# Rows of the modulation on the vector engine, and a router packed into column groups, in a two-layer diffusion backbone

## The chip, the cores and the metric

The kernel runs on one core of a Trainium2 chip. The metric is the device time of one execution in microseconds (us), from runs of the whole program; 0.2% of it are 5.8 us. TensorE (PE), VectorE (DVE), ScalarE (ACT), GpSimd (POOL) and SyncE (SP, which issues most transfers) each work through a queue of their own in order.

## The reference, cut to what matters

1024 latent tokens and 256 context tokens of 1024 features go through two layers. Each layer has six modulation rows per kind of token, a product of a vector with a 1024 by 6144 matrix (24 MB per layer), and an expert layer with 16 experts that each choose 128 latent tokens.

```
for layer in range(2):
    mod  = silu(c) @ mod_w[layer] + mod_b[layer];  sh1, sc1, g1, sh2, sc2, g2 = split(mod, 6)
    modc = silu(c_ctx) @ mod_w[layer] + mod_b[layer]         # the same for context tokens
    h = rms_norm(x, norm1_g) * (1 + sc1) + sh1               # rows 0 and 1
    y = conv_and_latent_attention(h) if layer == 0 else windowed_attention(h)
    x = x + g1 * (y @ w_out)                                 # row 2
    h2 = rms_norm(x, norm2_g) * (1 + sc2) + sh2              # rows 3 and 4
    aff = softmax(h2 @ router_w[layer])                      # 16 experts
    g, idx = top_k(aff.T, 128)
    x = x + g2 * scatter_add(idx, g * expert(h2[idx]))       # row 5
out = rms_norm(x, final_g)
```

In layer 1 the context tokens end with their keys and values, so their rows 2 to 5 of that layer are not needed.

## The kernel before, in words

The order of the work of every engine is written out by hand: inside `tc.manual_schedule` each queue holds its instructions in program order. float32 operands are split in a high and a low part, and `mm3` (line 162) makes three products of them (lines 163 to 165). Weights arrive in a ring of buffers, are copied to their high part by ScalarE, and the low part is a subtraction on VectorE (or GpSimd).

**Modulation.** A `Part` (class at line 277) makes two rows for both kinds of tokens on TensorE: for each of 8 pieces of 128 features (1 MB) four products into four groups of 32 columns (line 299). A `Row` (class at line 324) makes one row on VectorE: for each of four pieces of 256 features (1 MB) two multiply-adds over [128, 1024] per kind of tokens (line 348; the first is line 350), and at its end `sum` adds over the partitions with one product per half and kind, with a matrix of ones (line 356), an addition on VectorE, and a store by GpSimd. `modulations` merges the pieces of both into one generator: its first call loads two pieces ahead and each later one uses a piece and loads another. Before, `PARTS` are layer 0's rows 2 to 5 and layer 1's rows 0 and 1 for both kinds; `ROWS` are layer 1's rows 2 to 5 for latent tokens. Layer 0's rows 0 and 1 come ahead of the convolution.

**Convolution** (from line 559). Four chunks of 128 features, each with 15 projections of 256 tokens (24 products, lines 163 to 165): five groups of tokens by u, gate c and gate b. `proj` ends with one call of the generator, in all 54 calls for 44 pieces. After the last z (line 613) of a chunk VectorE has the taps (lines 579 to 581), the gates (line 585) as their projections end, and the low parts of the next chunk's weights (line 488), which the next chunk's first product reads.

**Output, router and route** (`mixer_out`, line 1252). Tiles of 128 tokens; a generator `steps(j)` puts pieces of tile j−1's router between tile j's products. `R` (line 1244) multiplies the tokens (128x128 weights) with 16 router columns, 8 products per tile. The softmax over all tiles (`softmax_experts`, line 1442) stands at the head of `route_x`, which finds each expert's 128 tokens with VectorE. `W.convert` (line 1084) splits expert weights ahead, on GpSimd where it is given `pool`.

**Layer 1's projections** (`layer1_mixer`, loop from line 1979). Ten tiles of 128 tokens, in the order of seven latent ones, context, latent, context. For each: the output of layer 0's last expert is added for the tile two on (`P`, `add`), with squares and the norm (lines 1876 to 1888, 172 to 189); the transposes and split of the next tile (`turn`, lines 393 and 1904); products `M` with three thirds of the weights, 24 products each (keys and values first), and the rotation of keys (`kv`) and queries (`q`, lines 1921 to 1925).

```
if j:
    x.M(range(8), 2)
    tiles[j - 1].q(1)
for y in x2:
    y.add(); y.sq(); y.norm()
x.kv()
if not x.s:                       # latent tokens
    if j: x.M(range(8), 0)
    x.q(0)
    if j: x.M(range(8), 1)
```

`early` (line 2233) brings layer 1's rows 0 and 1 onto the partitions inside an expert of layer 0, and the router's weights (`load_routers`, line 1418) with them.

Of the kernel before, what the change touches and what calls it, by code (L numbers as in the profile page):

```python
# [21 lines left out]
D = 1024  # L22
# [17 lines left out]
# one step of the software pipeline of an attention: (operation, how many steps late)  # L40
# [55 lines left out]
def hybrid_block_kernel(ctx, tc, A, out, dbg=None, upto=99):  # L96
# [13 lines left out]
    def psum(name, **tags):  # L110
        """PSUM of a phase: tag -> (buffers, banks each)"""
# [20 lines left out]
    act.copy(identb, ident)  # L132

    warm = const.tile([128, 1], F32, name="warm")

    def table(f, src=ones):
        """has the table of a function loaded ahead of its use"""
# [29 lines left out]
    def rstd_steps(pool_, ss, n, dim, tag, out=None):  # L167
        """1/sqrt(ss/dim + eps) for ss [128, n]: the root of dim times 1/sqrt(ss + dim*eps). A generator"""
# [42 lines left out]
    def scale_rows(pool_, l, s, i, g):  # L211
        """norm_g * (1 + sc) on all partitions"""
# [8 lines left out]
    def columns(c, n, scratch, tag):  # L221
        """n rows of D features with the features on partitions: c [128, row, 8]"""
# [4 lines left out]
    class Ring:  # L227
        """buffers for what is read from DRAM, in turn"""
# [4 lines left out]
        def more(self, raws):  # L233
            """further buffers, next in turn"""
# [11 lines left out]
    class Ahead:  # L246
        """the output projection of the first layer in four parts, the first of them split ahead"""
# [29 lines left out]
    class Part:  # L277
        """two of the rows, for latent and context tokens, 512 features at a time, summed by TensorE"""
# [45 lines left out]
    class Row:  # L324
        """one of the rows, for the kinds of tokens ss, summed by VectorE but over the partitions"""

        def __init__(self, c, l, r, ss, pool_):
            self.c, self.l, self.r, self.ss, self.pool = c, l, r, ss, pool_
            self.w = {}
# [10 lines left out]
        def use(self, k):  # L340
# [3 lines left out]
            for i in range(2):  # L344
                for s, a in zip(self.ss, self.acc):
                    cv = self.c[:, 2 * (k + i) + s:2 * (k + i) + s + 1]
# [5 lines left out]
        def sum(self):  # L352
            n = 64 * len(self.ss)
            pm, mb = bank("C", "pm"), self.mb
# [10 lines left out]

    def modulations(parts, rows, ahead):
        """a generator that stops after every piece of the weights, loaded some pieces ahead"""
# [19 lines left out]
    def transposes8(src, n=8):  # L387
        """eight [128,128] blocks of src (free) into two banks"""
# [8 lines left out]
    # ================= layer 0: projections =================  # L397
    def layer0_conv(hp, wp, cp):
        """first norm, input projection and short convolution"""
        hT = [[hp.tile([128, 8, 256], F32R, name=f"hT{g}_{i}") for i in range(2)] for g in range(5)]  # L400
        csil = hp.tile([128, 16], F32, name="csil")
# [9 lines left out]
        class Group:  # L411
            """256 tokens"""
# [14 lines left out]
            def norm(self):  # L427
                """a generator"""
# [16 lines left out]
            def T(self, b, tag="B"):  # L445
                """two blocks of 128 features of the normalized tokens, features on partitions"""
# [26 lines left out]
        class Chunk:  # L473
            """columns of the input projection, 256 features at a time"""
# [23 lines left out]
        def aside():  # L498
            """the next of the small operations that run between others"""
# [55 lines left out]
        rest = modulations([Part(cs, l, i, cp) for l, i in PARTS], [Row(csil, l, r, ss, cp) for l, r, ss in ROWS], 2)  # L555

        # short conv, 128 features at a time
        for j in range(4):
# [9 lines left out]
            def proj(f, g):  # L568
# [4 lines left out]
                if j or g > 1:  # L573
                    next(rest, None)
# [57 lines left out]
        if "conv" in dbg:  # L632
            for j in range(4):
                pool.dma_start(dbg["conv"][j], yTd[j])
        return hT, chunks[4], rest

    def latents(lp, hT, w, rest, kvT, kT, latT):
        """low-rank queries, keys and values, token-major, and their transposes"""
# [7 lines left out]
        class Latent:  # L646
# [18 lines left out]
            def norm(self):  # L665
                """a generator"""
# [59 lines left out]
    def layer0_mixer():  # L726
# [20 lines left out]
        with sbuf("l0a") as ap_, sbuf("l0t") as tp:  # L747
# [5 lines left out]
            class Head:  # L753
                """k^T and q^T of a head, in pieces of one bank"""
# [120 lines left out]
            with sbuf("l0b") as bp, psum("l0s", S=(2, 2), M=(1, 1), T=(2, 1), O=(1, 1)):  # L875
                class Pair:
                    """attention of 256 latent queries of one head, as the steps of MLA_ORDER"""
# [98 lines left out]
                class Few(Pair):  # L976
                    """attention of the 256 context queries of one head, to context keys only"""
# [72 lines left out]
    class Weights:  # L1050
        """expert weights of a layer in the order of their use: loaded ahead, split in two parts"""
# [43 lines left out]
    # ================= output projection, residual, second norm, router =================  # L1095
    class OutWeights:
        """the output projection in four parts, the first of them loaded ahead"""
# [20 lines left out]
        def first(self, y):  # L1118
            """the first tile of what the weights multiply, in two parts; y to hold it"""
# [1310 lines left out]
```

## Time and profile before

| | |
|---|---|
| median of three runs | 2921.93 us (2921.34 to 2925.74) |
| span of the profiled execution | 2924.6 us, granted TensorE clock 0.966 |
| TensorE busy | 2732.1 us (93%) |
| VectorE busy | 2126.5 us (73%) |
| ScalarE, GpSimd busy | 1609.2 us (55%), 443.8 us (15%) |
| DMA | 613.91 MB, mean 210 GB/s |

The profiled execution's own time is given by its span alone, from its first to its last instruction; it lies 2.7 us above the median of the runs. A line of a timeline gives the start, how long the instruction or group took, engine, line, operation, tiles and, in brackets, the idle time before it and what ended it. Matmuls overlap in their durations, so what one costs is read from the starts of its neighbours. The stages, by the timeline: convolution 40 to 264 us, latents to 310, latent attention to 655, output of layer 0 to 780, route to 845, experts of layer 0 to 1655, projections of layer 1 to 1840, windowed attention to 2142, output to 2257, route to 2305, experts of layer 1 to the end.

### The profile page before, as it was taken

What the parts mean: (1) busy time and instruction counts of PE and PEld (TensorE: products, weight loads), DVE (VectorE), ACT (ScalarE), POOL (GpSimd) and SP (SyncE); (2) the same over time, 40 slices, a digit from 0 to 9 for tenths busy, and PEclk for the clock granted to TensorE, in tenths of its full rate; (3) what the DMA queues carried; (4) which work ended last, traced back from release to release, by engine and by line L of the source; (5) the groups of instructions that cost most, each with busy time, mean ns of one, the idle gap of its engine ahead of it and who ended that gap; (6) DMA issues with size and microseconds to landing.
All of it is one profiled execution on the core that took longest, in us unless ns stands there. A gap on an engine that the chain in (4) does not pass through costs nothing. (4 is left out here: it accounts for less than half of the span.)

```text
span 2924.6 us, 43411 instructions
## 1 busy us (share of the span) xinstructions
PE 2732.1 (93%) x16999; PEld 2160.2 (74%) x16999; DVE 2126.5 (73%) x3298; ACT 1609.2 (55%) x2390; POOL 443.8 (15%) x293
## 2 busy tenths in 40 slices
PE   6999899999959999999999899899998599999996
PEld 5889899988746666666666678688877488877775
DVE  4653799986666666666666554799976688888887
ACT  4201577773225555555555543588943377776664
POOL 2100100000050111010011210232200622221103
PEclk8999999999979999999999999799999799999998
DMA  7782000016438878788888631310056599999994
GB/s 266 286 317 88 5 8 10 9 60 232 159 111 311 290 275 276 273 290 273 276 270 276 227 126 73 128 37 30 25 192 239 197 377 384 383 382 370 367 354 144
DMA packets 274637, 613.91 MB, mean 210 GB/s; under 512 B 25064, under 2 KB 72928, under 8 KB 270336
## 3 DMA queue, kind: packets, MB, share of 16 engines
q1 hardware_dynamic: 259408, 567.38, 54.2%
q0 software_dynamic: 14880, 43.62, 5.8%
q8 instruction: 134, 2.20, 0.3%
q14 instruction: 71, 0.58, 0.1%
q10 hardware_dynamic: 144, 0.13, 0.0%
HBM read 549.41 MB, written 61.67 MB: 209 GB/s over the span
## 5 line engine op out<-in xcount | busy, mean ns | idle before, releaser
L1081 DVE TENSOR_TENSOR wl<-raw,wh 128x2048 fp32r<-128x2048 f32 (+1 forms) x382 | 861.9, 2283 | 247.7 <-ACT wh L1080 247.6
L1080 ACT CAST wh<-raw 128x2048 fp32r<-128x2048 f32 (+1 forms) x392 | 735.5, 1903 | 260.9 <-PE pg L1723 150.2
L1719 PE MATMUL pg<-wl,xh 128*128 128x512 f32 x512 | 210.0, 410 | 3.6 <-ACT xh L159 2.9
L1721 PE MATMUL pu<-wl,xh 128*128 128x512 f32 x512 | 206.1, 402 | 5.3 <-DVE wl L1081 5.3
L1720 PE MATMUL pg<-wh,xh 128*128 128x512 f32 x512 | 203.2, 397 | 0.0
L1724 PE MATMUL pu<-wh,xl 128*128 128x512 f32 x512 | 202.5, 395 | 0.0
L1723 PE MATMUL pg<-wh,xl 128*128 128x512 f32 x512 | 201.8, 394 | 0.0
L1722 PE MATMUL pu<-wh,xh 128*128 128x512 f32 x512 | 201.6, 394 | 0.0
L1775 PE MATMUL pd<-wl,hh 128*128 128x512 f32 x480 | 197.1, 411 | 1.2
L1776 PE MATMUL pd<-wh,hh 128*128 128x512 f32 x480 | 194.0, 404 | 0.0
L1664 POOL DMA_INDIRECT xg<-h2x,gp x32 | 56.5, 1766 | 721.9 <-PE ptr L393 710.1
L1779 PE MATMUL pd<-wh,hl 128*128 128x512 f32 x480 | 151.2, 395 | 0.0
L1739 ACT ACTIVATE sil<-pg 128x512 f32<-128x512 f32 x64 | 38.3, 598 | 204.3 <-PE pg L1723 204.3
L163 PE MATMUL pc<-hT,wh 128*128 128x256 f32 x480 | 139.8, 291 | 5.5 <-ACT wh L487 3.8
L1789 POOL DMA_INDIRECT acc_x<-yo,gp x30 | 92.9, 3096 | 312.4 <-DVE yo L1788 302.2
L164 PE MATMUL pc<-hT,wh 128*128 128x256 f32 x480 | 135.0, 281 | 0.0
L165 PE MATMUL pc<-hT,wl 128*128 128x256 f32 x480 | 134.9, 281 | 0.0
L1719 PEld LDWEIGHTS pg<-wl,xh 128*128 128x128 f32 x512 | 96.5, 188 | 44.9 <-issue 21.6
L1736 PE MATMUL pcg<-raw,cT 128*32 128x256 f32 x2048 | 125.5, 384 | 0.5 <-DMA raw<-in_exp_w_up_dram 0.5
L1775 PEld LDWEIGHTS pd<-wl,hh 128*128 128x128 f32 x480 | 90.1, 188 | 43.6 <-issue 18.9
L1721 PEld LDWEIGHTS pu<-wl,xh 128*128 128x128 f32 x512 | 96.7, 189 | 32.8 <-DVE wl L1081 10.8
L943 ACT CAST pt<-ppt 128x512 fp32r<-128x512 f32 (+1 forms) x192 | 95.1, 516 | 39.0 <-PE ppt L936 36.8
(437 smaller groups left out, 6638.4 us busy)
## 6 DMA issues: line engine op xcount, KB each, us to landing
raw<-in_exp_w_gate_dram SPq DMA_DIRECT2D x128, 1024.0 KB
raw<-in_exp_w_up_dram SPq DMA_DIRECT2D x128, 1024.0 KB
raw<-in_exp_w_down_dram SPq DMA_DIRECT2D x128, 1024.0 KB
raw<-in_mod_w_dram SPq DMA_DIRECT2D x48, 1024.0 KB
yT<-yTd SPq DMA_DIRECT2D x17, 512.0 KB
acc_x<-xn SPq DMA_DIRECT2D x16, 512.0 KB
h2x<-h SPq DMA_DIRECT2D x16, 512.0 KB
raw<-in_w_in_dram SPq DMA_DIRECT2D x8, 768.0 KB
```

The lines of the kernel that those rows point to most:

```text
L163: pe.matmul(o, ah, bl, start=first, stop=False)
L1080: act.copy(wh[:, cs], raw[:, cs])
L1081: (eng or dve).tensor_sub(wl[:, cs], raw[:, cs], wh[:, cs].bitcast(F32))
L1719: pe.matmul(pg, xh[:, k], gl[:, j], start=k == 0, stop=False)
L1720: pe.matmul(pg, xh[:, k], gh[:, j], start=False, stop=False)
L1721: pe.matmul(pu, xh[:, k], ul[:, j], start=k == 0, stop=False)
L1722: pe.matmul(pu, xh[:, k], uh[:, j], start=False, stop=False)
L1723: pe.matmul(pg, xl[:, k], gh[:, j], start=False, stop=k == 7)
L1724: pe.matmul(pu, xl[:, k], uh[:, j], start=False, stop=k == 7)
L1775: pe.matmul(pd[n], hh[k // 4][:, k % 4], w[2][:, k % 2, ns], start=k == 0, stop=False)
L1776: pe.matmul(pd[n], hh[k // 4][:, k % 4], w[1][:, k % 2, ns], start=False, stop=False)
L1779: pe.matmul(pd[n], hl[k // 4][:, k % 4], w[1][:, k % 2, ns], start=False, stop=k == 7)
```

## The change

Layer 0's rows 2 to 5 leave TensorE for VectorE in the convolution, for both kinds of tokens, and pieces come at every second projection (28 pieces in 29 calls). Layer 1's rows 2 to 5 move from the convolution to layer 1's projections, with up to three calls a tile and one load ahead; two tiles of the ring's second pool are lent as accumulators. The router's weights become the stationary operand, padded to 32 columns, in four column groups; a product `F` with `fold` adds the four and transposes. Each tile's softmax follows at once. Two of GpSimd's splits in each route move: in layer 0 one to the route's head and one to VectorE behind it, in layer 1 two of four to VectorE behind it. Layer 1's router weights are loaded and scaled in layer 1's output stage.

```diff
-PARTS = [(0, 1), (0, 2), (1, 0)]
-ROWS = [(1, r, (0,)) for r in (2, 3, 4, 5)]
+PARTS = [(1, 0)]
+ROWS = [(0, r, (0, 1)) for r in (3, 4, 2, 5)]
+ROWS_NEXT = [(1, r, (0,)) for r in (3, 4, 2, 5)]
...
                 if j or g > 1:
-                    next(rest, None)
+                    calls[0] += 1
+                    if calls[0] % 13 % 2 == 0:
+                        next(rest, None)
...
         def R(self):
+
+            p = bank("B", "plT")
+            for k in range(8):
+                q = k % 4 * 32
+                pe.matmul(p[q:q + 32, :128], self.o.router[self.s][:, k], self.xT[:, k], start=k < 4, stop=k >= 4)
+            self.lT = self.wp.tile([128, 128], F32, tag="rb", bufs=2, name="lT")
+            act.copy(self.lT, p[:, :128])
+
+        def F(self):
+
             lg = self.o.lg
             if self.s not in lg:
                 lg[self.s] = bank("C", "lg")
-            c0 = self.i * E
-            for k in range(8):
-                pe.matmul(lg[self.s][:, c0:c0 + E], self.xT[:, k], router[self.o.l, self.s][0][:, k], start=k == 0, stop=k == 7)
+            self.lg = lg[self.s][:, self.i * E:(self.i + 1) * E]
+            pe.matmul(self.lg, self.lT, fold, start=True, stop=True)
+
+        def soft(self):
+
+            a = self.o.aff[self.s][:, self.i, :]
+            m, d = [self.wp.tile([128, 1], F32, tag=t, bufs=2, name=t) for t in ("rm", "rd")]
+            dve.scalar_tensor_tensor(a, self.lg, self.o.rr[self.s][:, self.i:self.i + 1], router[self.o.l, self.s][1],
+                                     op0=ALU.mult, op1=ALU.add)
+            dve.tensor_reduce(m, a, axis=AX.X, op=ALU.max, negate=True)
+            act.activation(a, a, AF.Exp, bias=m, accum_out=d)
+            dve.reciprocal(d, d)
+            dve.tensor_scalar(a, a, d, None, op0=ALU.mult)
...
+                for _ in range(4):
+                    next(m0)
+                    yield
+                y.F()
+                if not y.s:
+                    y.soft()
                 yield from m0
...
-                elif l == 0:
-                    W.convert(1, pool)
...
                 rest = steps(8)
-                take(rest, 15)
+                take(rest, 20)
 
                 def more():
+                    yield
+                    W.convert(1, pool)
                     yield from rest
...
                     yield from rest
-                    for _ in range(4):
-                        for _ in range(12):
-                            yield
+                    for _ in range(2):
+                        yield
                         W.convert(1, pool)
                         W.load(1)
...
             run(fill)
+            if l:
+                W.convert(2)
+                W.load(2)
             if l == 0:
-                W.convert(1, pool)
+                W.convert(1)
...
+                lender = next(p for p, _ in ring.raws if p is not raw0)
+                ring.less(lender)
+                lent = Lent(lender.tile([128, 2, D], F32, tag="raw", bufs=2, name="lent"))
+                rest = modulations([], [Row(l, r, ss, lent, "B") for l, r, ss in ROWS_NEXT], 1)
...
+                    if j:
+                        steps(rest, 1)
                     x.kv()
+                    if j > 1:
+                        steps(rest, 1 if j < TT - 1 else 99)
...
                         x.q(0)
                         if j:
+                            steps(rest, 1)
                             x.M(range(8), 1)
```

## Rows read from the trace of the kernel before

**Rows 1.** Windows: convolution, layer 1's projections; us, busy us per engine, granted clock, DMA share, GB/s.

```profile
40.00:264.00 224.00, 222.24 (x1774) 192.93 (x1775) 126.00 (x247) 44.15 (x84) 20.99 (x31) 0.98 0.65 237
...
1655.00:1840.00 185.00, 171.43 (x762) 136.70 (x760) 95.51 (x231) 80.89 (x150) 16.16 (x12) 0.96 0.33 119
```

**Rows 2.** Windows of 10 us, 1700 to 1830, summed over all thirteen.

```profile
sum 130.00, PE 130.00 PEld 106.22 DVE 66.33 ACT 53.67 POOL 2.71; mean PE 10.00 PEld 8.17 DVE 5.10 ACT 4.13 POOL 0.21
```

**Rows 3.** Timeline of TensorE, convolution, a part's group; start us, us (ends modelled).

```profile
143.75 0.28 PE L165 MATMUL pc<-hT,wl 128*128 128x256 f32 x1
143.96 1.07 PE L299 MATMUL pm<-raw,cs 128*32 128x512 f32 x8
...
145.18 0.28 PE L164 MATMUL pc<-hT,wh 128*128 128x256 f32 x1
```

**Rows 4.** Timeline of TensorE, convolution, the closing sum of a row.

```profile
154.75 1.05 PE L356 MATMUL pm<-modacc,ones 128*32 128x512 f32 x4
...
155.95 0.28 PE L164 MATMUL pc<-hT,wh 128*128 128x256 f32 x1
```

**Rows 5.** Timeline of VectorE, end of the first chunk.

```profile
95.41 0.43 DVE L613 TENSOR_TENSOR z<-pc,gcs 128x256 f32<-128x256 f32 x1 [0.65 <-PE pc L165]
...
105.33 2.60 DVE L348 SCALAR_TENSOR_TENSOR modacc<-raw,csil,modacc 128x1024 f32<-128x1024 f32 x2
107.85 1.82 DVE L488 TENSOR_TENSOR wl<-raw,wh 128x768 fp32r<-128x768 f32 x2
```

**Rows 6.** Timeline of VectorE, layer 1's projections: norms' last operations, keys' rotation.

```profile
1766.92 0.16 DVE L189 TENSOR_SCALAR y<-y 128x1 f32<-128x1 f32 x1
1768.83 0.43 DVE L1921 TENSOR_TENSOR kr<-ks,tb 128x256 f32<-128x256 f32 x1 [1.75 <-ACT ks L1929]
...
1802.89 0.15 DVE L189 TENSOR_SCALAR y<-y 128x1 f32<-128x1 f32 x1
...
1817.89 0.15 DVE L189 TENSOR_SCALAR y<-y 128x1 f32<-128x1 f32 x1
```

**Rows 7.** Timeline of TensorE, layer 1's projections: products where the sums will stand.

```profile
1767.18 0.39 PE L163 MATMUL pqkv<-wl,hh 128*128 128x512 f32 x1
...
1797.60 0.39 PE L163 MATMUL pqkv<-wl,hh 128*128 128x512 f32 x1
...
1820.67 0.39 PE L163 MATMUL pqkv<-wl,hh 128*128 128x512 f32 x1
```

**Rows 8.** Timeline of TensorE, start of layer 1's projections, idle and pitch.

```profile
1665.94 1.97 PE L393 MATMUL ptr<-ident,xr 128*128 128x128 f32 x8 [4.23 <-ACT xr L1888]
1669.36 0.79 PE L163 MATMUL pqkv<-wl,hh 128*128 128x512 f32 x1 [1.45 <-ACT hh L1903]
...
1675.08 0.44 PE L164 MATMUL pqkv<-wh,hh 128*128 128x512 f32 x1
```

**Rows 9.** Timeline of TensorE, layer 0's output, the router's products.

```profile
708.15 1.85 PE L1250 MATMUL lg<-rA,xT 128*128 128x16 f32 x16
...
710.17 0.40 PE L1194 MATMUL pw<-wl,yh 128*128 128x512 f32 x1
```

**Rows 10.** Timeline of TensorE, an expert's products in column groups.

```profile
1007.63 1.07 PE L1783 MATMUL pcd<-raw,chT 128*32 128x256 f32 x16
```

**Rows 11.** Timelines of VectorE and GpSimd, layer 0's route.

```profile
810.55 0.21 DVE L1547 TENSOR_TENSOR rc<-rc 32x64 f32<-32x64 f32 x1
...
810.93 4.42 DVE L1547 TENSOR_TENSOR rc<-rc 32x64 f32<-32x64 f32 x1
...
810.71 4.57 POOL L1081 TENSOR_TENSOR wl<-raw,wh 128x2048 fp32r<-128x2048 f32 x1 [193.47 <-ACT wh L1080]
```

**Rows 12.** Timelines of VectorE and GpSimd, layer 1's route.

```profile
2260.96 1.45 DVE L1461 TENSOR_TENSOR raff<-raff,rm 128x128 f32<-128x128 f32 x1
...
2278.75 4.42 DVE L1539 COPY rb<-rval 64x128 f32<-64x128 f32 x1
...
2265.18 17.91 POOL L1081 TENSOR_TENSOR wl<-raw,wh 128x2048 fp32r<-128x2048 f32 x4 [0.49 <-ACT wh L1080]
```

More of the change, by code (lines that the diff above doesn't have):

```diff
@@ L364, in units, with __init__, tile @@
             return [(partial(self.load, k), partial(self.use, k)) for k in range(0, 8, 2)] + [(None, self.sum)]
+    class Lent:
+        def __init__(self, raw):
+            self.tiles = {"modacc0": raw[:, 0], "modbr": raw[:, 1, :512]}
+        def tile(self, shape, dtype, tag, **_):
+            return self.tiles[tag]
     def modulations(parts, rows, ahead):
@@ L554, in layer0_conv @@
         sp.dma_start(cw, A["convp"])
-        rest = modulations([Part(cs, l, i, cp) for l, i in PARTS], [Row(csil, l, r, ss, cp) for l, r, ss in ROWS], 2)
+        rest = modulations([Part(cs, l, i, wp) for l, i in PARTS], [Row(l, r, ss, cp) for l, r, ss in ROWS], 2)
+        calls = [0]
         for j in range(4):
@@ L634, in layer0_conv @@
                 pool.dma_start(dbg["conv"][j], yTd[j])
+        steps(rest, 99)
         return hT, chunks[4], rest
@@ L1136, in __init__, with pad @@
             self.rr = {s: rp.tile([128, TX], F32, tag="rr", bufs=2, name="rr") for s in range(2)}
+            self.aff = {s: p.tile([128, n, E], F32, tag=f"raff{s}", name="raff") for s, n, p in ((0, TX, wp), (1, TC, rp))[:2 - l]}
+            self.router = {}
+            if l == 0:
+                self.pad()
+        def pad(self):
+            l, wp = self.l, self.wp
+            for s in self.aff:
+                r = self.router[s] = wp.tile([128, 8, 32], F32, tag=("rpair", "rP1")[s], name="rP")
+                dve.memset(r[:, :, E:], 0.0)
+                dve.tensor_copy(r[:, :, :E], router[l, s][0])
         def weights(self, c):
@@ L1258, in mixer_out @@
             o.first = tiles[0]
+            routers = iter(())
+            if l:
+                routers = load_routers("B", l, (0,), wp.tile([128, 8, 128], F32, tag="xn", bufs=2, name="scratch"))
             def run(g):
@@ L1279, in mixer_out @@
             o.scale_load(0)
+            next(routers, None)
             tk = wp.tile([128, 418], F32, name="tk")
@@ L1308, in steps @@
                         yield from x.M(1, ks)
+                        if l and ks[0] >= 2:
+                            next(routers, None)
+                    if l:
+                        o.pad()
                     x.xn(0)
@@ L1359, in last @@
                 y.R()
+                y.F()
+                if not y.s:
+                    y.soft()
                 yield
@@ L1405, in mixer_out @@
                     y.store()
-                g = softmax_experts(wp, o.lg[1], o.rr[1], TC, 0, 1)
-                while 1 not in routed:
-                    try:
-                        next(g)
-                    except StopIteration as done:
-                        routed[1] = done.value
+                for y in tiles[8:]:
+                    y.soft()
+                routed[1] = o.aff[1]
                 table(AF.Silu)
@@ L1523, in route_x @@
             yield
-        pair = wp.tile([128, 128, 2], F32, name="rpair")
+        pair = wp.tile([128, 128, 2], F32, tag="rpair", name="rpair")
         act.copy(pair[:, :, 0], val)
@@ L1756, in moe @@
                 if e == 1 and early:
-                    early()
+                    steps(early(mp.tile([128, 128], F32, name="ecol")), 9)
                 if e + 1 < E:
```

48 lines of the change are left out of this document (14 added, 34 removed).

## Prediction

> **What bounds the kernel now.** I read the windows by stage first. In the convolution stage TensorE works 222.2 of 224 us at a granted clock of 0.98, and in layer 1's projections 171.4 of 185 us [rows 1]; within the latter, from 1700 to 1830 us, it is busy 130.00 of 130 us while VectorE is busy 66.3 [rows 2]. So in both stages every TensorE instruction taken away or added counts in full, and VectorE has room on average. Whether it has room at the right moment only the order within a tile can tell, so I read the timelines of both engines next. The route stages, where TensorE waits, are read on VectorE and GpSimd.
>
> **A1. Convolution: products removed.** Two parts leave, eight pieces each, so 16 groups of 4 column products. From one product ahead of a group to the second behind it are 145.18 − 143.75 = 1.43 us [rows 3], of which two products' pitch of 0.117 are 0.23: a group costs 1.20 us. 16 × 1.20 = **−19.2 us**. The four closing sums of VectorE's rows stay four; they now have both kinds of tokens, which fill four column groups where two were used. One costs 0.02 less than a part's group, 155.95 − 154.75 against 145.18 − 143.96 [rows 3, 4], so 1.18 us, and with four groups 1.20: no change.
>
> **A2. Convolution: VectorE's units double.** One unit (two k-steps, one kind of tokens) takes 2.52 us (105.33 to 107.85) [rows 5], with two kinds 5.1. Behind it on VectorE's queue stands the split of the next chunk's weights (its first half is out 0.91 us after 107.85), and TensorE needs that after the four last projections of the chunk, 4 × 24 × 0.117 = 11.2 us after z is ready (95.41), plus what parts lie between. Before, the split came 13.4 us after z while TensorE had 11.2 plus two or so groups, 13.6: no wait. After, with every second call, two units lie in a tail: 13.4 + 2 × 2.55 = 18.5, against 11.2 + one group or sum of 1.2 and some slack where z comes early. I take waits of 4.1 and 4.9 in chunks 1 and 2 and 0.3 in chunk 3, where one unit fewer is in the tail: **+9.3**, from 0 (the units fall between the tails) to +14 (a third full wait). Waits of this length can halve the clock: after waits of 4.23 and 1.45 us the 13 products from 1669.36 to 1675.08 took 5.72 us, 0.44 each, the pitch of the lower level (1.2 GHz), instead of 0.23 [rows 8]; beside the entry of the first, 2.6 us were lost. For two waits 0 to 5, I take 4. Net of A1 and A2: −19.2 + 9.3 + 4 = **−6**, from −19 to 0. The 16 MB that leave here free a queue that nobody waits for: nothing.
>
> **A3. Layer 1's projections: what is added.** Twenty pieces enter: 16 units of 2.55 us on VectorE (41 us, within its 64 idle us from 1700 to 1830) and four sums on TensorE, 4 × 1.18 = **+4.7**. Their loads go through SP and a ring of three buffers; one megabyte at a time each is issued a unit ahead, and the transfers of the stage leave two thirds of the queue time free [rows 1]: 0, up to 2. But a sum stands in TensorE's queue at a fixed place and reads the accumulator that VectorE's unit just before it finishes. The first call only loads, then units follow at up to three places in a tile: before the keys, behind them and behind the first query half. So the sums fall at: row 1 before the keys of tile 3 (its unit is a place back, no wait), row 2 behind the queries' first half of tile 4, row 3 behind the keys of tile 6, row 4 behind those of tile 8. All these units stand behind the norm of the tile two on, a chain of nine small operations that itself waits for ScalarE's squares.
> - Tile 4: the norm ends 1767.08, one unit then 1769.65; the keys' rotation (at 1768.83, a multiplication of 0.43, and two more steps: 1.3) then 1770.9, second unit 1773.5 [rows 6]. TensorE is done with what precedes the sum at 1767.2 [rows 7]: it waits 6.3.
> - Tile 6: the norm ends 1803.04, plus a unit 1805.6, against 1797.6: waits 8.0 [rows 6, 7].
> - Tile 8: the norm ends 1818.04, plus three units 1825.7, against 1820.7: waits 5.0 [rows 6, 7].
>
> These are 19.3 us. Carried forward through the stage (each unit also delays the rotations, the weights' and tokens' low parts and so the next norm), the three become 7.3, 8.5 and 7.1, **+22.9**. Behind the waiting sum stand the tile's next 24 products, which nothing else on TensorE can replace. Clock: each wait is longer than the pair in [rows 8], which cost 2.6; 0 to 2.6 each, I take 1.4: **+4**. Stage: 4.7 + 22.9 + 4 = **+32**, from +5 (no waits) to +36.
>
> **B. Router kept in the array.** R is now 16 records of 16 columns, 1.79 us a tile: 710.17 − 708.15 = 2.02, less one product of 0.23 [rows 9]. After, 8 products of 128 columns in four column groups, two sets. The nearest row, 16 records of 256 columns in two sets, takes 1.07 [rows 10]; with half the columns, about 0.55 and the entry and exit 0.2: 0.77; then F, one product with 128-row weights, two records, 0.3. Saved about 0.7 a tile, from 0 (sets that don't overlap) to 1.0. Fourteen of 18 tiles lie where TensorE is the bound: 14 × 0.7 = **−9.6**, from 0 to −14. ScalarE's copy of the logits hides under the four products that follow; without them it would cost 0.5 a tile.
>
> **C. Softmax by tile.** Each tile gets five small operations of VectorE and ScalarE, 1.5 us, ahead of the residual. TensorE gives that slot 5 us of products, so 0 (up to +0.3 a tile). At the route's head seven operations go; one of them, normally 0.3, was held 1.45 us by GpSimd [rows 12]. −1.5 per route, counted in D.
>
> **D. Splits moved.** Layer 0: GpSimd's split of 4.57 at 810.71 held VectorE's maximum at 810.93 for 4.42 instead of 0.21 [rows 11]; a second split held another for 1. After, the first is at the route's head and the second is VectorE's own, 2.3, behind the route. What will the early one hold? The 128-wide sorting ran undisturbed beside GpSimd in layer 1, but the copy at 2278.75 took 4.42 [rows 12]; no row here shows the residual's addition of two SBUF operands beside a GpSimd split. Between 0 and 4.4, nearest to the row of 810.93 (also two SBUF operands), I take 3.5: −5.2 + 3.5 + 2.3 − 1.5 = **−1**, from −5 to +3. The Trainium skill, "SBUF — State Buffer", section "Who interferes with whom", says that an operation of VectorE with two SBUF inputs and a GpSimd one that reads SBUF exclude each other for the whole length of the one that began. By it the early split could hold the residual for all of its 4.57 and the term be 0; by the sorting's rows alone, which GpSimd didn't disturb, it would hold nothing and the term be −4.5. No row here shows that very pair. Layer 1: four splits of 17.91 us held the copy and a scalar operation (about 1.6) as well as the softmax's last (1.2) [rows 12]. Two early ones leave at most one of these, two go to VectorE behind the route, where it waits for gathers: about −5 − 1.5, and +0.5 for two loads that now collide with the gathers: **−6**, from −9 to 0.
>
> **E. Router weights of layer 1** move from an expert to the output's first tile: −0.5 there; four more transfers on SP ahead of the route table, transposes between products, +1 if their rows are late (0 to 2). **+0.5.** The first chain of the last stage, transfers of the experts' weights at the memory's rate, takes any earlier or later start in full.
>
> **Sum.** −6 (A1, A2) + 32 (A3) − 9.6 (B) − 1 and −6 (D, with C) + 0.5 (E) = **+10 us** on the profiled execution, whose span is 2924.6 us: 2934.6. The span lies 2.7 above the median of the runs, 2921.93, so I give **2932** on that scale.
>
> **Rivals.**
> 1. *VectorE is there in time* (faster). If a row's last unit ends before TensorE reaches its sum, A3 is 4.7 and a few us for shifts. That decides at tile 6: the unit would have to end by 1797.6, 8 us before my reading. For it: VectorE is idle half of this stage [rows 2]. Against it: units follow the norm on a queue kept in order. Then −6 + 8 − 9.6 − 7 + 0.5 = −14: **2908**.
> 2. *Waits without their tail* (about even). No clock is lost and nothing is carried forward: A2 −9.9, A3 4.7 + 19.3 = 24: −9.9 + 24 − 9.6 − 7 + 0.5 = −2: **2920**. For it: carrying forward is the softest step. Against: the waits are each longer than those that cost 2.6 in [rows 8].
> 3. *Clock and convolution both at their upper bounds* (slower still). Every wait costs 2.6 more, a third tail waits, B saves half: 0 + 36 − 5 − 5 + 1 = +27: **2949**.
> 4. *B does not do what it says*: column groups don't overlap for these products. Then B is 0 and the sum +20: 2942; against it speaks [rows 10], where 16 records in groups fit in 1.07.
>
> **How the numbers follow.** 0.2% (5.8 us) is about what a measurement of this kernel can tell from no change. The forecast gets 0.41, rival 1 0.26 (the order of two queues is read from one tile pattern), rival 2 0.18, rivals 3 and 4 0.15. Faster by over 0.2% (below 2916): rival 1 and a fifth of rival 2, 0.30. Within: the rest of rival 2 and a little of the forecast, 0.18. Slower: the rest, 0.52. The likeliest case alone spans 2926 to 2940; the range for 8 in 10 runs from 2904, below rival 1, to 2948, up to rival 3.
>
> **What would show it.** Right: TensorE idle in the layer 1 projections at the sums of tiles 4, 6 and 8, 5 to 9 us each, released by VectorE's accumulator; half-clock products behind them; 128 records instead of 256 of the parts' products; waits for the weights' low part in two conv tails; R near 0.8; four instead of ten splits on GpSimd and no 4.4 us copy in layer 1. Wrong: the sums at tiles 4, 6 and 8 start without a wait, or the projections' stage grows by under 15 us. Then A3 falls, and the sign with it.

## The result, and the profile after

The changed kernel takes 2949.14 us (median of four runs, 2948.76 to 2949.55) against 2921.64 for the kernel before beside it (2920.75 to 2925.74): a ratio of 1.0089, interval 1.0075 to 1.0102, so 27.5 us slower where 10 were forecast. The sign and the stage that pays are as forecast; by its ratio the time is 2947.9 on the prediction's scale, just inside the stated range of 2904 to 2948. The profiled execution's own time is 2948.91 us, its span 2947.1, 22.5 more than the span before; the profiled execution of before was the slow end of its runs, which is most of the other 5 us.

Where the time went is read from TensorE's timeline: the start of the first product of each stage in both traces (for the table of lists, of VectorE's `flat`, line 1594 before), and from these the length of each stage.

| stage, first product to first product | before, us | after, us | difference |
|---|---|---|---|
| convolution | 226.7 | 219.1 | −7.6 |
| latents and latent attention | 404.4 | 405.5 | +1.1 |
| output of layer 0, up to the table of lists | 160.4 | 147.6 | −12.8 |
| that table to the first expert product | 13.5 | 16.6 | +3.2 |
| experts of layer 0 | 827.8 | 826.2 | −1.6 |
| **projections of layer 1** | 195.1 | 233.1 | **+38.0** |
| windowed attention | 278.0 | 277.9 | −0.2 |
| output of layer 1, up to the table | 153.2 | 151.4 | −1.8 |
| that table to the first expert product | 10.3 | 15.2 | +4.9 |
| experts of layer 1 | 600.5 | 601.9 | +1.3 |

Unrounded, with 1.7 us that the convolution begins earlier, this sums to +22.9. The windows of the two stages, convolution and projections (start and end, us, then busy us and instructions of TensorE, its weight loads, VectorE, ScalarE and GpSimd, granted clock, DMA share, GB/s):

```profile
40.00:254.00 214.00, 207.50 (x1655) 193.41 (x1654) 153.68 (x270) 41.72 (x80) 19.84 (x29) 0.97 0.49 168
1636.00:1858.00 222.00, 180.24 (x774) 138.98 (x772) 131.45 (x267) 80.82 (x150) 17.65 (x15) 0.92 0.50 174
```

In the second, TensorE, which was busy for 171.43 of 185 us before [rows 1], is now idle for 42 of 222. The two largest groups of its waits there, 1645 to 1860 us (waiting tile, what ended it: us in total, times, longest):

```profile
PE pm L361 <- DVE lent L353: 28.2, 4, 10.4
PE pqkv L168 <- POOL wl L1883: 4.8, 1, 4.8
```

The first group is the four sums waiting for VectorE's accumulator, the waits that the prediction placed; the waits for the weights' low parts, of which the second is one, came to 3.6 us before. On TensorE's timeline (start, us, instruction, in brackets the wait and its releaser):

```profile
1722.92 1.05 PE L361 MATMUL pm<-lent,ones 128*32 128x512 f32 x4 [0.88 <-DVE lent L353]
1758.60 1.92 PE L361 MATMUL pm<-lent,ones 128*32 128x512 f32 x4 [10.41 <-DVE lent L353]
1760.45 0.80 PE L168 MATMUL pqkv<-wl,hh 128*128 128x512 f32 x1
...
1762.64 0.39 PE L170 MATMUL pqkv<-wh,hl 128*128 128x512 f32 x1
...
1800.00 1.92 PE L361 MATMUL pm<-lent,ones 128*32 128x512 f32 x4 [7.92 <-DVE lent L353]
1834.90 1.92 PE L361 MATMUL pm<-lent,ones 128*32 128x512 f32 x4 [8.98 <-DVE lent L353]
```

Row 1's sum hardly waits; the other three wait 10.4, 7.9 and 9.0 us (forecast 6.3, 8.0 and 5.0 read directly). Behind each, the products start 0.43 apart, the lower clock level (1.2 GHz), and then 0.23: five products from 1760.45 to 1762.64, and four and ten behind the last two sums. VectorE at the same place:

```profile
1742.13 2.60 DVE L353 SCALAR_TENSOR_TENSOR lent<-raw,csil,lent 128x1024 f32<-128x1024 f32 x2 [4.87 <-DMA raw<-in_mod_w_dram]
...
1752.07 0.15 DVE L194 TENSOR_SCALAR y<-y 128x1 f32<-128x1 f32 x1
1752.14 2.59 DVE L353 SCALAR_TENSOR_TENSOR lent<-raw,csil,lent 128x1024 f32<-128x1024 f32 x2
1754.65 0.42 DVE L1962 TENSOR_TENSOR kr<-ks,tb 128x256 f32<-128x256 f32 x1
1755.85 2.60 DVE L353 SCALAR_TENSOR_TENSOR lent<-raw,csil,lent 128x1024 f32<-128x1024 f32 x2
```

The order is the one that the prediction read for tile 4: norm, unit, the keys' rotation, unit, sum. From the norm's end (1752.2) to the sum are 6.4 us, as forecast (1767.08 to 1773.5). What is new is the first line: an earlier unit waited 4.87 us for its megabyte, so the norm ended 4 us after TensorE was ready (1748.2), where before the two fell together [rows 6, 7]. From 1700 to 1840 us this group of VectorE's waits is:

```profile
DVE lent L353 <- DMA raw<-in_mod_w_dram: 13.3, 7, 4.9
```

The router's products in layer 0's output, and layer 1's route on GpSimd and VectorE:

```profile
711.58 0.39 PE L1223 MATMUL pw<-wh,yh 128*128 128x512 f32 x1
711.90 0.64 PE L1278 MATMUL plT<-xT,rP 128*32 128x128 f32 x16
...
712.81 0.39 PE L1223 MATMUL pw<-wl,yh 128*128 128x512 f32 x1
...
713.50 0.29 PE L1288 MATMUL lg<-fold,lT 128*128 128x16 f32 x2
```

```profile
2290.46 8.97 POOL L1098 TENSOR_TENSOR wl<-raw,wh 128x2048 fp32r<-128x2048 f32 x2
2312.73 2.85 POOL L1640 DMA_INDIRECT gp<-lists,flat  x1 [13.30 <-DVE flat L1635]
2321.24 0.97 POOL L1705 DMA_INDIRECT xg<-h2x,gp  x1 [5.67 <-issue]
...
2298.09 1.42 DVE L1567 TENSOR_SCALAR rpair<-rids,tk 128x128 int32<-128x128 uint32 x1
...
2312.36 4.49 DVE L1098 TENSOR_TENSOR wl<-raw,wh 128x2048 fp32r<-128x2048 f32 x2
...
2312.58 2.46 SPq L1088 DMA_DIRECT2D raw<-in_exp_w_up_dram  x2
```

The router's products (R) take 712.81 − 711.58 less two products of 0.23: 0.77, against 1.79 before [rows 9]. In the route the copy that took 4.42 [rows 12] is undisturbed, and the two early splits hold one operation for 1.42. But the lookup of the lists (line 1640) takes 2.85 where it took 1.04, and the gather starts 8.5 us after the start of the lookup instead of 3.6 (2299.76 − 2296.15 before): beside it now stand VectorE's splits and SP's new loads.

### The profile page after: what moved, and what is told of

It reads as the page before. It is cut to its first block, busy times and chain, and to the rows that moved or that the text cites. A ratio compares the mean times of both kernels' runs of the same rounds, so it can differ in the third digit from the quotient of the medians.

```text
span 2947.1 us, 43462 instructions
## 1 busy us (share of the span) xinstructions
PE 2719.1 (92%) x16939; PEld 2144.5 (73%) x16939; DVE 2201.3 (75%) x3425; ACT 1618.4 (55%) x2441; POOL 432.1 (15%) x294
## 5 line engine op out<-in xcount | busy, mean ns | idle before, releaser
L1098 DVE TENSOR_TENSOR wl<-raw,wh 128x2048 fp32r<-128x2048 f32 x385 | 868.2, 2282 | 249.8 <-ACT wh L1097 249.7
L1760 PE MATMUL pg<-wl,xh 128*128 128x512 f32 x512 | 211.2, 412 | 5.0 <-ACT xh L164 4.5
L170 PE MATMUL pc<-hT,wl 128*128 128x256 f32 x480 | 137.8, 287 | 4.8 <-DVE wl L501 4.8
L1760 PEld LDWEIGHTS pg<-wl,xh 128*128 128x128 f32 x512 | 96.7, 189 | 46.9 <-issue 23.2
L1762 PEld LDWEIGHTS pu<-wl,xh 128*128 128x128 f32 x512 | 96.6, 189 | 33.3 <-DVE wl L1098 10.4
```

The costliest lines, as they stand in the source:

```text
L1098: (eng or dve).tensor_sub(wl[:, cs], raw[:, cs], wh[:, cs].bitcast(F32))
L1760: pe.matmul(pg, xh[:, k], gl[:, j], start=k == 0, stop=False)
L1762: pe.matmul(pu, xh[:, k], ul[:, j], start=k == 0, stop=False)
```

## The experiments

Each is an edit of the changed kernel unless it says otherwise; ratios are to the kernel before, on the same chip. How far a long stage varies by itself shows where a run leaves it as it is: against before, the projections of layer 1 came out at +36.9 to +40.3 us in the changed kernel and runs 6 to 8, the experts of layer 0 at −1.6 to +0.8 in the changed kernel and runs 1, 2 and 6 to 8. Differences of up to some 3 us in the one and 2 in the other say nothing.

**1. The sums one place later.** Each sum of a layer-1 row is put one call behind its last unit.

```diff
+            gap = [(None, lambda: None)] if self.tag == "B" else []
-            return [(partial(self.load, k), ...) for k in range(0, 8, 2)] + [(None, self.sum)]
+            return [(partial(self.load, k), ...) for k in range(0, 8, 2)] + gap + [(None, self.sum)]
```

> The changed kernel, but in layer 1's projections an empty place stands ahead of each of the four closing sums, so that a sum comes one place later than the unit it reads (the last one behind the keys of the last tile). Theory (TensorE waits at the sums for VectorE): the waits of 28.2 us that the changed kernel's profile shows at the sums fall to at most 3 us in all, and with them the half-clock stretches behind them; units and transfers stay the same. Time 2949 - 28 - 4 = 2917 us, 2912 to 2923. Rival (the units' load on VectorE and on the transfers slows the stage, whatever the place of the sums): 2940 to 2949 us, with the waits moved to other products.

Measured: 2919.66 us, ratio 0.9976 (0.9966 to 0.9986). The stage is 5.9 us longer than before instead of 38.0, and the sums' waits are

```profile
PE pm L361 <- DVE lent L353: 4.8, 4, 2.5
```

The time is as expected. So the products, units and loads that the stage gained are nearly free; the place of the sums is what cost 32 us. VectorE still waits 9.4 us for the loads here, in six places, and the stage hardly pays for it.

**2. One more load ahead.** The same units and sums, with two megabytes on their way.

```diff
-rest = modulations([], [Row(l, r, ss, lent, "B") for l, r, ss in ROWS_NEXT], 1)
+rest = modulations([], [Row(l, r, ss, lent, "B") for l, r, ss in ROWS_NEXT], 2)
```

> The changed kernel with the weights of layer 1's rows loaded two units ahead instead of one. The changed kernel's VectorE waits 13.3 us for these loads in seven places. Theory (the loads, which I had set at 0 to 2 us, lengthen the waits at the sums from the forecast 22.9 to 28.2): VectorE's waits for them fall under 3 us, TensorE's at the sums to 21 to 25, the time 4 to 7 us below the changed kernel's. Rival (the sums wait for the norms ahead of their units in any case): the sums' waits stay above 27 us.

Measured: 2941.25 us, ratio 1.0062 (1.0045 to 1.0078). VectorE's waits for these loads are gone, the stage is 27.3 us longer than before instead of 38.0, and the sums wait

```profile
PE pm L361 <- DVE lent L353: 19.1, 3, 7.9
```

That is the 19.3 us that the prediction read directly from the order of the two queues, and each of the three waits (6.3, 8.0 and 5.0 read) is met as well:

```profile
1756.23 1.92 PE L361 MATMUL pm<-lent,ones 128*32 128x512 f32 x4 [6.10 <-DVE lent L353]
...
1797.46 1.92 PE L361 MATMUL pm<-lent,ones 128*32 128x512 f32 x4 [7.92 <-DVE lent L353]
...
1828.36 1.92 PE L361 MATMUL pm<-lent,ones 128*32 128x512 f32 x4 [5.07 <-DVE lent L353]
```

With the sums at their place, the late loads are worth 10.7 us of the stage, some 8 us by the two ratios.

**3. Rows where they were.** `PARTS`, `ROWS` and a call at every projection as before, no `ROWS_NEXT`; router, softmax and splits as changed.

```diff
-PARTS = [(1, 0)]
-ROWS = [(0, r, (0, 1)) for r in (3, 4, 2, 5)]
-ROWS_NEXT = [(1, r, (0,)) for r in (3, 4, 2, 5)]
+PARTS = [(0, 1), (0, 2), (1, 0)]
+ROWS = [(1, r, (0,)) for r in (2, 3, 4, 5)]
+ROWS_NEXT = []
```

> The changed kernel with the modulation rows as before: layer 0's rows 2 to 5 on TensorE, layer 1's on VectorE beside the convolution, a piece at every projection, none in layer 1's projections. Theory (the rows' move costs 30 us: 37.6 more in layer 1's projections, 7.6 less in the convolution): 2949 - 30 = 2919 us, 2915 to 2924. Rival (router, softmax and splits carry the loss): 2935 us or more.

Measured: 2922.36 us, ratio 0.9985 (0.9976 to 0.9995). The projections are at −1.8, so the 38 us belong to the rows. But the convolution came out 4.8 us longer than before with the same groups and no new wait: its products are further apart. Something else that the change brings costs 4.8 there; if the two simply added, the rows' move alone would be −7.6 − 4.8 = −12.4. The next two runs look for it.

**4. Constants off the head of the memory.** The change adds two small tiles, `csil` and `fold` (together 128 bytes a partition), ahead of everything in SBUF. Here they live elsewhere, so that TensorE's other operands should have the addresses that they had before.

```diff
-    fold = const.tile([128, E], F32, name="fold")
...
-    csil = const.tile([128, 16], F32, name="csil")
...
+        csil = col["c"] = hp.tile([128, 16], F32, name="csil")
...
+                sp.dma_start(lent.c, csd)
```

> The changed kernel with the two new constants (64 bytes of a partition each) taken from the head of SBUF: the vector of the modulation stands where it stood before, a copy for layer 1 in the lent tile, and fold behind the output stage's tiles, so that every operand of TensorE in the convolution and the experts has its address of before. In the changed kernel all of these lie 128 bytes further on, and products of 256 columns in the convolution come 0.120 us apart instead of 0.117, those of layer 0's experts 0.233 instead of 0.229. Theory (the address sets this pitch): both pitches return, convolution 4.7 us shorter, output stages 2, experts 4: 11 us off the changed kernel, so 14 to 19 us above the kernel before instead of 27. Rival (the pitch comes from the instruction stream or from the chip that ran it): the pitches stay at 0.120 and 0.233, the time within 2 us of the changed kernel's.

**5. The kernel before, shifted by 128 bytes.** An unused constant is all that is added.

```diff
+    const.tile([128, 32], F32, name="pad")
     warm = const.tile([128, 1], F32, name="warm")
```

> The kernel before with one unused constant of 128 bytes at the head of SBUF, which moves the tiles behind it by 128 bytes and changes no instruction. Theory (address): 0.120 in the convolution and 0.233 in layer 0's experts, 9 to 14 us slower than the kernel before. Rival (instruction stream): no change, within 2 us.

Measured: run 4 2949.65 us, ratio 1.009 (1.0073 to 1.0107), as slow as the change; run 5 2933.45 us (2929.31 to 2940.88), 1.0034 (1.0021 to 1.0047), some 8 to 10 us slower than before by nothing but an unused tile. The pitch shows it. In the convolution, second and last product of the same 24 in the changed kernel, in run 4 and in run 5:

```profile
64.29 0.28 PE L169 MATMUL pc<-hT,wh 128*128 128x256 f32 x1
...
66.93 0.29 PE L170 MATMUL pc<-hT,wl 128*128 128x256 f32 x1
```

```profile
65.60 0.28 PE L168 MATMUL pc<-hT,wh 128*128 128x256 f32 x1
...
68.19 0.29 PE L169 MATMUL pc<-hT,wl 128*128 128x256 f32 x1
```

```profile
64.40 0.28 PE L165 MATMUL pc<-hT,wh 128*128 128x256 f32 x1
...
66.97 0.27 PE L166 MATMUL pc<-hT,wl 128*128 128x256 f32 x1
```

22 steps take 2.64, 2.59 and 2.57 us. In an expert of layer 0, eleven steps of the kernel before and of run 5:

```profile
917.02 0.39 PE L1720 MATMUL pg<-wh,xh 128*128 128x512 f32 x1
...
919.54 0.39 PE L1719 MATMUL pg<-wl,xh 128*128 128x512 f32 x1
```

```profile
916.82 0.40 PE L1720 MATMUL pg<-wl,xh 128*128 128x512 f32 x1
...
919.38 0.39 PE L1725 MATMUL pu<-wh,xl 128*128 128x512 f32 x1
```

2.52 and 2.56 us, 0.229 and 0.233 a product. Putting the constants elsewhere brings the pitches back: in the mean of neighbouring starts (0.09 to 0.16 us apart in the convolution, 0.20 to 0.27 in the experts), 0.117 against 0.120 in the convolution, and 0.2296 against 0.2333 in the gate and up products (`pg`, `pu`) of layer 0's experts. Their down products (`pd`) go the other way: 0.2333 in the kernel before and 0.2331 in run 4, but 0.2303 in run 5 and 0.2299 in the changed kernel, so the shift widens some products and narrows others. The chip isn't the cause, for run 2 was measured on the same one as runs 4 and 5 and has the changed kernel's pitches; nor, in the experts, are the instructions, which run 5 leaves as they are.

Yet in run 4 the convolution gains 1.6 us only and the experts of layer 0 0.6. In the convolution other losses take the place of the wider pitch: TensorE waits longer for VectorE's low parts (5.5 us instead of 4.8) and 1.0 for tokens, and its products start 0.21 apart behind both of the tails' waits, where they do so behind one in the changed kernel. In run 10, where the pitch is narrow too, the convolution is at −7.6 as in the changed kernel. So the effect on the pitch is shown and its price in this kernel is not: my 11 us were wrong, and by the totals it is nothing, give or take some 6 us. With the narrow pitch, the rows' move is worth −9.3 (run 4) to −7.6 (run 10) in the convolution, not −12.4. In run 5 the expert stages pay 2.8 and 3.0 us and the output of layer 1 2.9, but the convolution keeps its pitch of 0.117; why, no run here shows.

**6. The router's products as before.** Softmax by tile and all else stays.

```diff
-            p = bank("B", "plT")
-            for k in range(8):
-                q = k % 4 * 32
-                pe.matmul(p[q:q + 32, :128], self.o.router[self.s][:, k], self.xT[:, k], start=k < 4, stop=k >= 4)
...
+                pe.matmul(lg[self.s][:, c0:c0 + E], self.xT[:, k], router[self.o.l, self.s][0][:, k], start=k == 0, stop=k == 7)
```

> The changed kernel with the router's products as before (128 tokens as weights, 16 columns moving, 16 records a tile), the softmax by tile kept. Theory (each tile's 1.79 against 0.77 + 0.22 us counts in full where TensorE is the bound): 14 tiles x 0.8 = 11 us slower than the changed kernel, 38 above the kernel before, 35 to 41. Rival (the output stages are bound by VectorE's chain of the tile): within 3 us of the changed kernel's 27.

Measured: 2961.32 us, ratio 1.0125 (1.0109 to 1.014), 0.36% or 10.5 us above the changed kernel. By stages the outputs are 5.6 (layer 0) and 6.1 us (layer 1) longer, and in the latter 1.1 of it is a longer wait for the router's rows (6.9 instead of 5.8 us): part B is worth 10.5 to 12 us.

**7. Layer 1's router rows ahead of the first tile.** In the changed kernel the rows' loads stand on SP's queue behind the first tile's. One of them, 4 KB, takes 4.84 us to issue behind several of half a megabyte, and TensorE's transpose waits for it:

```profile
2167.24 4.84 SPq L224 DMA_DIRECT2D scratch<-modr  x1
```

```profile
2177.01 0.27 PE L229 MATMUL pcol<-ident,scratch 24*128 24x24 f32 x1 [5.79 <-DMA scratch<-modr]
```

```diff
             if l:
+                next(routers)
                 tiles[0].yh, tiles[0].yl = w_out.y
...
             o.scale_load(0)
-            next(routers, None)
```

> The changed kernel with the four transfers of layer 1's router rows issued ahead of the other transfers of the output stage instead of behind five of half a megabyte. Theory (TensorE waits 5.8 us for these rows at the first tile, and loses 3 more at half clock behind it): both go, 2949 - 8 = 2941 us, 2938 to 2944. Rival (the wait only passes to the rows that now come behind, or the clock falls there anyway): 2946 to 2949 us.

Measured: 2945.86 us, ratio 1.006 (1.0044 to 1.0077). From layer 1's output to the table of lists the stage is 6.2 us shorter than before instead of 1.8, so 4.4 of the 8 expected. The wait for `scratch` is gone and a shorter one has come:

```profile
PE prb L1502 <- DVE scratch L1497: 3.0, 1, 3.0
```

**8. The new loads behind the first gather** (layer 1; the splits stay).

```diff
             if l:
                 W.convert(2)
-                W.load(2)
...
+                if l == 1:
+                    sp.dma_start(qd[0:1, :], xgs[0][0:1, :])
+                    W.load(2)
```

> The changed kernel, but in layer 1's route the loads of two megabytes behind VectorE's two splits wait for the first gather of tokens (a small transfer reads its tile ahead of them); the splits stay. Rival A (the loads take the transfer engines from the lookup and the gather): the gather's rows land 4 to 5 us earlier, as before, 2944 us. Rival B (VectorE's splits, two operands from SBUF, hold GpSimd's descriptors of the lookup up): the lookup still starts 5 us late and the time stays within 1 of 2949 us.

Measured: 2949.7 us, ratio 1.0073 (1.0056 to 1.009); a total can't show 3 us here, the stage can: from the table to the first expert product it is 2.0 us longer than before instead of 4.9. The lookup is as slow as it was, and the gather starts sooner behind it:

```profile
2317.62 2.85 POOL L1639 DMA_INDIRECT gp<-lists,flat  x1 [13.30 <-DVE flat L1634]
2323.13 0.97 POOL L1704 DMA_INDIRECT xg<-h2x,gp  x1 [2.67 <-issue]
```

So 2.9 of the 4.9 us come from the loads; of the 2.0 that stay, the slower lookup is 1.8, and it has another cause.

**9. Runs 1, 4 and 7 together, and layer 1's two splits left to the first expert.** Here `W.convert(2)` and `W.load(2)` behind the route go too.

> The changed kernel with the constants at home, the sums one place later, the router's rows first, and layer 1's last two splits left to the first expert (behind its tokens' split). If the parts add: against the changed kernel's 27 us above the kernel before, 34 off for the sums' place, 8 for the rows, 4 for the gather, 11 for the addresses: 30 us below the kernel before, 22 to 34. Rival (parts overlap, the early splits are missed by the first expert): less than 20 below.

Measured: 2915.94 us, ratio 0.9969 (0.9956 to 0.9981), 9 us below before instead of 30. The splits, now issued on demand, ran on VectorE in the middle of the sorting, beside GpSimd's:

```profile
2258.16 3.79 DVE L1101 TENSOR_TENSOR wl<-raw,wh 128x2048 fp32r<-128x2048 f32 x1
2262.60 5.85 DVE L1101 TENSOR_TENSOR wl<-raw,wh 128x2048 fp32r<-128x2048 f32 x1
```

```profile
2255.28 11.02 POOL L1101 TENSOR_TENSOR wl<-raw,wh 128x2048 fp32r<-128x2048 f32 x2
2285.66 1.06 POOL L1643 DMA_INDIRECT gp<-lists,flat  x1 [19.36 <-DVE flat L1638]
```

The last line answers run 8: with no split on VectorE behind the route the lookup takes 1.06 again, although one load still stands beside it. The 2.85 are the splits' doing. The kernel before has the same among its 32 lookups: the 22 with under 0.7 us of VectorE's splits beside them take 0.94 to 1.06 us, the ten with more than 1 us of them 1.90 to 3.00, as here:

```profile
2315.84 2.72 POOL L1599 DMA_INDIRECT gp<-lists,flat  x1 [0.30 <-issue]
...
2315.45 4.49 DVE L1081 TENSOR_TENSOR wl<-raw,wh 128x2048 fp32r<-128x2048 f32 x2 [8.03 <-ACT wh L1080]
```

From the table to the first expert product run 9 is still 2.1 us longer than before: with that one load GpSimd idles 4.7 us between the lookup and the gather, where it was 2.6 before.

**10. Runs 1, 2, 4, 7 and 8 together.**

> The changed kernel with the constants at home, the sums one place later, the rows' weights loaded two units ahead, the router's rows first, and layer 1's loads behind the first gather (its two splits on VectorE stay where the changed kernel has them). From the stages of the single runs against the kernel before: convolution -9, layer 0's output and route -10, first experts -2, projections +2 to +6, output of layer 1 -4, route -7 and +2, last experts +1: 25 us below the kernel before, 18 to 30. Rival (leaving the splits to the first expert was no loss, and the sums' remaining waits are the norms'): no better than the run with all of it but this, 9 us below.

Measured: 2905.36 us (2902.49 to 2906.51), ratio 0.9932 (0.9919 to 0.9946), 19 us below the kernel before (25 expected) and, by the two ratios, some 46 below the changed one: faster than both. By stages against before: convolution −7.6, output of layer 0 to the table −12.4, from there to the first expert product +3.2, experts of layer 0 −4.1, projections +4.6, output of layer 1 to the table −6.1, from there to the first expert product +2.0. One short wait is left at the sums:

```profile
PE pm L360 <- DVE lent L352: 2.5, 1, 2.5
```

## Why the prediction was right in its sign and short in its size

| part | forecast, us | measured, us | from |
|---|---|---|---|
| A1, A2 convolution | −6 | −7.6 | stages; −9.3 with the narrow pitch (run 4) |
| A3 projections | +32 | +38.0 | stages |
| B router | −9.6 | −11.7 | run 6, stages; −10.5 by the totals |
| C, D layer 0 | −1 | −4.0 | −12.8 + 3.2 + 5.6 of B |
| C, D layer 1 | −6 | −1.7 | output's last product to the table −6.6, table to the first expert +4.9 |
| E layer 1's router rows | +0.5 | +11.0 | output alone +4.9, with B's −6.1 in it |
| elsewhere | 0 | −1.1 | the stages that are left |

The sum is +22.9 on the profiled spans, 13 more than forecast: E (10.5), A3 (6.0) and layer 1's D (4.3) were put too low, and layer 0's D, B and the convolution came out better by 3.0, 2.1 and 1.6.

**A1 and A2** came right by luck, by errors that cancel. Two tails wait, as said, but 4.8 us in all (`PE pc L170 <- DVE wl L501`) instead of 9.3. The clock fell behind one of the two waits only: behind the first, of 2.43 us, the granted clock is 1.00 (155 to 158 us), behind the second, of 2.33 us, it is 0.51 (206.5 to 209.5), and 13 products start 0.21 apart; that is about 2 us and not 4. The wider pitch, which nothing in the trace of before could show and which cost 4.8 in run 3, took back most of what these saved.

**A3**, the largest step, failed in size, and the failed term is the one for the rows' loads ("0, up to 2"). I had reasoned that two thirds of the queue time are free and that a load is issued a unit ahead. VectorE waited 13.3 us for these loads, and run 2 prices them at 10.7. But the units stand in clusters of up to three a tile, as close as 3.7 us (1752.14 and 1755.85), and a load that is issued one unit ahead has that long to arrive. A mean share of the queue says nothing on that. The rest holds: with the loads in time the sums wait 6.1, 7.9 and 5.1 us, read directly as 6.3, 8.0 and 5.0. The amount carried forward (22.9) wasn't needed for it; that it is nearer to the total of 28.2 is luck. The clock's part is close to the forecast: of 38.0, the waits are 28.2 and the sums 4 × 1.18 = 4.7, which leaves 5.1 for three sums at 1.85 instead of 1.18 and the slow products behind them; 4 were forecast. That waits at the sums are the cause and not the work itself is shown by run 1, where even VectorE's 9.4 us of waits for the loads cost next to nothing: they count where a sum stands right behind its last unit.

**B** is right: 0.77 for R as estimated, F 0.22 (713.27 to the second product behind at 713.95, less two products) instead of 0.3, and 10.5 to 12 us in all.

**D, layer 0.** The early split did hold the residual's addition, for 3.6 us; I had taken 3.5:

```profile
769.83 4.52 POOL L1098 TENSOR_TENSOR wl<-raw,wh 128x2048 fp32r<-128x2048 f32 x1 [160.30 <-DVE rids L1563]
...
770.60 4.30 DVE L1232 TENSOR_TENSOR xn<-xn,xt 128x512 f32<-128x512 f32 x1
```

The median of its twenty is 0.692. It ends 0.55 us behind GpSimd's split. The Trainium skill, "SBUF — State Buffer", section "Who interferes with whom", has it so (two SBUF inputs on VectorE, a GpSimd operation that reads SBUF, the second one blocked until the first is done). The trace agrees: 4.30 us beside the split. The delay was paid, too: VectorE's sorting goes on behind the addition only, at 774.82, and TensorE waits for the addition:

```profile
775.04 0.63 PE L1266 MATMUL pxT<-ident,xn 128*128 128x128 f32 x4 [4.15 <-DVE xn L1232]
```

The stage up to the table is shorter by 7.2 beyond B nevertheless, for a reason that the forecast lacked. From the transposed affinities (`paf`) to the table VectorE takes 39.7 us instead of 46.0, and of its waits there this one nearly went (before, and after):

```profile
DVE xn L1202 <- PE pw L1194: 3.5, 1, 3.5
DVE xn L1231 <- PE pw L1223: 0.2, 1, 0.2
```

More of the output's products now stand ahead of the route (20 pieces of work instead of 15 in the diff's `take`); that this is why the wait went was not tried alone. Of the 3.2 that the way from the table to the first expert product gives back, 1.8 are a lookup of 2.85 us there too; most of the rest is a longer wait for ScalarE's copy of the tokens (`PE pg L1760 <- ACT xh L164`, 4.5 us instead of 2.9), which stands behind the exponentials of the context tokens' softmax.

**D, layer 1.** The step that failed is "+0.5 for two loads that now collide with the gathers", and that the two splits on VectorE were put at nothing there. The gain up to the table is 6.6, as summed; behind it 4.9 are lost, 2.9 to the loads (run 8), and of the 2.0 that are left without them 1.8 to the lookup, slowed by VectorE's splits (runs 8 and 9).

**E** failed by most, 10.5 us. "+1 if their rows are late" was a wait of 5.8 us for a load that took 4.84 to issue, and a stretch at the lower clock level behind it (26 instructions of TensorE in 8 us at a granted clock of 0.67). Run 7 got 4.4 of the 11 back. In the rest are the remaining wait of 3.0 us and the wider pitch of the output's products (0.232 instead of 0.229; the stage is 1.0 us shorter in run 4); its parts weren't separated, and some of it stays open.

**The rivals.** The first (VectorE in time) falls with the waits; run 1 shows that it needed only one place more. The second falls with the clock behind them, but its other half, that nothing is carried forward, is what run 2 shows. The fourth falls with R's 0.77. The third's 2949 was met, but not in its way: the convolution waits less and B saves in full, while the loads, E and layer 1's route, which its sum had not, made up for it.

## What to carry to other kernels

When work is moved to an engine with room, look at the one instruction on the in-order bottleneck engine that reads its result: put it a place behind the last unit, since a mean of idle time says nothing on the moment. Price the moved loads by the shortest distance between two units that use them, not by the queue's share; here they cost 10.7 us with the sums at their old place and next to nothing with the sums one place later. And what is put behind a routing step runs beside its lookups and gathers, where a few microseconds of loads and splits land on the path (2.9 and about 1.8 us in layer 1).

## What the runs showed of the hardware that I had not expected

- An unused 128-byte constant at the head of SBUF slowed the kernel before by 0.34% (0.21 to 0.47%). Products of 512 columns in layer 0's experts went from 0.2295 to 0.2333 us apart (gate and up) and from 0.2333 to 0.2303 (down); the changed kernel's convolution had 0.120 instead of 0.117 for products of 256 columns. Which operand's address decides was not settled.
- GpSimd's indirect lookup took 2.85 us when VectorE's subtractions of two SBUF operands ran beside it, and 1.04 to 1.06 when none did (kernel before and run 9); within the kernel before, 1.90 to 3.00 against 0.94 to 1.06.
- One 4 KB load took 4.84 us to issue on SP's queue, behind several of half a megabyte; its neighbours took 0.3 to 1.2.
- Of two waits of TensorE of nearly the same length in the convolution, 2.43 and 2.33 us, only the second was followed by the lower clock level (granted 1.00 and 0.51).
